# Layer 0 of a hybrid encoder: projections in split form, and additions and products given to GpSimd

## The chip, the cores and the metric

The kernel runs on one core of a Trainium2 chip. The core's engines work side by side, each on its own queue of instructions in a fixed order: TensorE (PE in the profile, with its weight loads as PEld) does matrix products, VectorE (DVE) and ScalarE (ACT) work element by element, GpSimd (POOL) can do so too and issues DMAs, SyncE (SP) issues DMAs. An instruction waits at the head of its engine's queue until what it needs is there, and everything behind it waits with it. The metric is the device time of one execution in microseconds (us); lower is better.

## The reference

Two layers over 272 tokens (16 meta tokens and 256 of the input), width 2048. Layer 0 is where the change lies.

```python
for layer in range(DEPTH):                      # 2
    hn = rms_norm(h, mix_norm[layer])
    proj = hn @ w_in[layer]                     # 2048 -> 512 + 256 + 64 + 1024
    c_q, c_kv, k_rope, u = jnp.split(proj, splits, axis=-1)
    att = mla_attention(c_q, c_kv, k_rope, ...) # 8 heads; c_q, c_kv are normed first
    ssm = s5_mixer(u, ...)                      # 64 groups of 16, 64 complex states, both ways
    mixed = jnp.concatenate([rms_norm(att, ...), rms_norm(ssm, ...)], axis=-1)
    h = h + mixed @ w_out[layer]
    hn = rms_norm(h, ffn_norm[layer])
    h = h + (swiglu(hn, ...) if layer % 2 == 0 else moe_swiglu(hn, ...))
...
def rms_norm(x, g):
    y = xf * lax.rsqrt(jnp.mean(xf * xf, axis=-1, keepdims=True) + EPS)
    return (y * g).astype(x.dtype)
```

All data are float32, and the result has to be near that precision.

## The kernel before, in words

Everything is kept transposed: a tile has 128 features on the partitions and the 272 tokens along the row. `h` is 16 such tiles. A matrix product of width 128 out runs over 16 weight tiles of 128x128, which come in blocks of eight (512 KB, one DMA by SyncE) through the class `Stream`.

A product has one of two forms. In the **raw form** the float32 block itself is the weight: one float32 matmul for each weight tile, which the trace shows as two instructions (`bank<-fa,raw`). In the **split form** the block is taken apart first: `Stream.high` rounds it on ScalarE into `wh` (type float32r), `Stream.low` takes the rest on VectorE into `wl`; the input is taken apart in the same way into `XH` and `XL`, and each weight tile then costs three float32r matmuls, `XH,wh`, `XL,wh` and `XH,wl` (the loop in `gemm`). Before the change the first 40 blocks of layer 0 (`NRAW`) are raw: all of the input projection and of the latents' projections. The rest of the kernel is in split form.

Layer 0's mixer (`mixer(0, ...)`) goes like this.

- **Prologue.** For each of the 16 tiles of `h`, ScalarE writes `X0` (h times the norm's gain) and the square of h (`sq_acc`); TensorE multiplies `X0` with the first two output tiles' weights and adds the square to a sum over all features with a product by a matrix of ones (`bank<-sqr,ones`). The sum gives `r_in`, by which every projection is scaled afterwards.
- **Projections.** 15 output tiles: 8 for `u` (two of them done in the prologue), 4 for c_q, 2 for c_kv, 1 for k_rope. In the text they are tile 1 to tile 15. `u` goes by GpSimd's DMAs to DRAM (`uscr`) and comes back in another layout.
- **S5.** `prep` works out powers of lambda on VectorE and transposes them on TensorE into `Wp`. `v_all` makes 16 batches of V: GpSimd issues three loads for a batch (two from `pscr`, one from `ssm_bT`), two batches ahead in a ring of three, VectorE makes V in four operations (`v_make`), TensorE multiplies V with `u` (`ssm_x`, 128x136 in the trace, four instructions for a group, 32 groups in all). Then `ssm_scan` runs 66 steps on VectorE. `w_all` makes 32 batches of W: five products and differences with `Wp` and one closing operation on VectorE, then a small product on TensorE (`toep`, shown as eight instructions with out 128x96 or 64x96) and three short additions. GpSimd loads `ssm_C` and `ssm_bz` for them.
- **The rest.** Heads and attention, the first half of `w_out`, the S5 output, the gated product (GLU) with its own sum of squares, the second half of `w_out`.

The order of all instructions is fixed when the kernel is built: generators hand out work, and a planner (`Model`, `Sched`) with costs for TensorE, VectorE, ScalarE and the DMAs decides when each is due by its own clock. `yield "w0"` means: go on when VectorE is at most 1350 ns ahead of TensorE by that clock. What the planner assumed wrongly shows as a wait in the queues.

## Time and profile before

| what | value |
|---|---|
| median of 3 runs | 2502.1 us (2499.97 to 2502.74) |
| profiled execution, its time | 2502.09 us |
| its span, first to last instruction | 2500.3 us |
| TensorE busy | 2424.5 us (97%) |
| VectorE busy | 1902.1 us (76%) |
| ScalarE busy | 1397.1 us (56%) |
| GpSimd busy | 151.4 us (6%) |

The profiled execution is the span and 1.8 us around it, and it stands at the median of the runs. Busy shares are over the whole span. Layer 0's mixer is the first seventh of it.

### The profile page before, as it was taken

The numbers are of one execution on the slowest core, as the hardware profiler recorded it, in microseconds if no ns is written. First come the engines' busy times: TensorE is split into PE (matmuls) and PEld (weight loads), VectorE is DVE, ScalarE is ACT, GpSimd is POOL, SyncE is SP. The second block draws the span as 40 slices with busy tenths as digits, with TensorE's granted clock in tenths as the row PEclk, the third lists the DMA queues.
The fourth block names the chain that finished last, engine by engine and source line by source line (L and its number), as shares of the span: only waits on it lengthen the run. The fifth ranks groups of instructions, "written<-read, shape, count | busy, mean of one in ns | idle before, by whom it ended". The sixth has DMA issues, their size and how long they took to land. (4 is left out here: it accounts for less than half of the span.)

```text
span 2500.3 us, 42271 instructions
## 1 busy us (share of the span) xinstructions
PE 2424.5 (97%) x15930; PEld 2189.2 (88%) x15930; DVE 1902.1 (76%) x3250; ACT 1397.1 (56%) x1908; POOL 151.4 (6%) x262
## 2 busy tenths in 40 slices
PE   8899999999999999999999899999999999999997
PEld 6675699999999999999998769997888888888886
DVE  8788667787766666555653887658999999999997
ACT  4424555443333333333458456646777877877775
POOL 3400100011100000000011002000000000000000
PEclk9999999999999999999999899999999999999998
DMA  7842554478765655555565316557999999999995
GB/s 257 238 145 83 155 155 160 161 223 273 245 197 189 193 190 176 184 169 177 178 199 174 125 44 220 220 191 263 391 351 352 383 340 375 363 329 373 362 336 198
DMA packets 192919, 583.47 MB, mean 233 GB/s; under 512 B 36225, under 2 KB 48897, under 8 KB 191553
## 3 DMA queue, kind: packets, MB, share of 16 engines
q1 hardware_dynamic: 174802, 520.42, 59.7%
q0 software_dynamic: 17040, 57.97, 7.6%
q8 instruction: 127, 2.08, 0.3%
q10 hardware_dynamic: 864, 2.28, 0.3%
q14 instruction: 86, 0.70, 0.1%
HBM read 560.14 MB, written 22.54 MB: 233 GB/s over the span
## 5 line engine op out<-in xcount | busy, mean ns | idle before, releaser
L408 DVE TENSOR_TENSOR wl<-raw,wh 128x1024 fp32r<-128x1024 f32 (+1 forms) x559 | 667.3, 1202 | 222.9 <-ACT wh L408 198.1
L408 ACT ACTIVATE wh<-raw 128x1024 fp32r<-128x1024 f32 (+1 forms) x559 | 579.4, 1040 | 309.6 <-PE bank L408 223.6
L408 PE MATMUL bank<-XH,wh 128*128 128x272 f32 (+1 forms) x2160 | 639.0, 296 | 0.8 <-ACT tmpr L408 0.5
L408 PE MATMUL bank<-XH,wl 128*128 128x272 f32 (+1 forms) x2160 | 624.7, 289 | 3.5 <-DVE wl L408 3.5
L408 PE MATMUL bank<-XL,wh 128*128 128x272 f32 (+1 forms) x2160 | 623.3, 289 | 1.5 <-DVE XL L408 1.3
L408 PEld LDWEIGHTS bank<-XH,wh 128*128 128x128 f32 x2160 | 410.1, 190 | 5.4 <-ACT tmpr L408 0.7
L408 PEld LDWEIGHTS bank<-XH,wl 128*128 128x128 f32 x2160 | 409.4, 190 | 4.2 <-DVE wl L408 4.2
L408 PEld LDWEIGHTS bank<-XL,wh 128*128 128x128 f32 x2160 | 410.2, 190 | 2.5 <-DVE XL L408 2.1
L408 PE MATMUL bank<-ra,wh 128*128 128x272 f32 (+1 forms) x1792 | 344.7, 292 | 2.3 <-ACT wh L408 2.3
L408 PEld LDWEIGHTS bank<-ra,wh 128*128 128x128 f32 x1792 | 283.7, 190 | 7.8 <-issue 3.1
L408 PE MATMUL bank<-fa 128*68 128x64 f32 (+11 forms) x1892 | 254.6, 273 | 30.7 <-DMA fa<-uscr 10.9
L408 PEld LDWEIGHTS bank<-fa 128*68 128x68 f32 (+6 forms) x1892 | 190.7, 157 | 88.6 <-issue 50.2
L408 DVE TENSOR_TENSOR fa<-fa 128x128 f32<-128x128 f32 (+9 forms) x687 | 236.3, 353 | 39.3 <-ACT fa L408 16.5
L408 PE MATMUL bank<-ra,wl 128*128 128x272 f32 (+1 forms) x896 | 258.4, 288 | 0.7 <-DVE wl L408 0.7
L408 ACT ACTIVATE fa<-bank 64x268 f32<-64x268 f32 (+9 forms) x313 | 159.3, 515 | 155.1 <-PE bank L408 136.2
L408 PE MATMUL bank<-wh,XH 128*128 128x512 f32 (+1 forms) x584 | 222.7, 381 | 0.4 <-ACT fa L408 0.4
L408 PE MATMUL bank<-wh,XL 128*128 128x512 f32 (+1 forms) x584 | 220.3, 377 | 0.0
L408 PE MATMUL bank<-wl,XH 128*128 128x512 f32 (+1 forms) x584 | 219.2, 375 | 0.0
L408 PE MATMUL bank<-wh,ra 128*128 128x512 f32 x552 | 185.1, 392 | 0.0
L408 PEld LDWEIGHTS bank<-ra,wl 128*128 128x128 f32 x896 | 170.4, 190 | 1.0 <-DVE wl L408 1.0
L408 PE MATMUL bank<-fa,raw 128*128 128x272 f32 x608 | 162.0, 404 | 7.8 <-DMA raw<-w_mix 6.3
L408 DVE TENSOR_TENSOR wl<-h,wh 128x1024 fp32r<-128x1024 f32 (+1 forms) x137 | 157.0, 1156 | 10.0 <-ACT wh L408 7.4
(127 smaller groups left out, 3211.3 us busy)
## 6 DMA issues: line engine op xcount, KB each, us to landing
raw<-w_dense SPq DMA_DIRECT2D x264, 512.0 KB, 3.6
raw<-w_mix SPq DMA_DIRECT2D x150, 512.0 KB, 3.8
raw<-w_moe_g SPq DMA_DIRECT2D x106, 512.0 KB, 5.6
h<-w_moe_g SPq DMA_DIRECT2D x80, 512.0 KB, 7.1
raw<-w_moe_d SPq DMA_DIRECT2D x73, 512.0 KB, 6.9
h<-w_moe_d SPq DMA_DIRECT2D x59, 512.0 KB, 6.7
raw<-w_moe_t SPq DMA_DIRECT2D x51, 384.0 KB, 4.0
h<-w_moe_t SPq DMA_DIRECT2D x44, 384.0 KB, 4.0
```

What stands on the lines that cost most here:

```text
L408: return f(*a, **k)
```

## The change

`NRAW = 40` becomes a list, `RAW`: blocks 0 to 5 (tiles 1 to 3) and 30 to 39 (the projections out of the latents, with the heads) stay raw, blocks 6 to 29 (tiles 4 to 15) are split. So ScalarE now rounds `X0` into `XH` and GpSimd takes the rest into `XL`, 16 operations each (`parts`), and 24 weight blocks are taken apart. The squares of h are no longer summed by TensorE one by one: GpSimd adds them into `wacc` (`joiner`), and one product with ones follows (`total`). In the same way VectorE joins the squares of the two latents and of the GLU's result. The five products and differences that make a batch of W go from VectorE to GpSimd; the closing operation and the three short additions stay (`VT`). The planner gets a time for GpSimd's operations, `pool_cost`, and the turn `"pool"`: go on when GpSimd is at most 1500 ns ahead. The DMAs that GpSimd issues are still planned on another clock.

```diff
-NRAW = 40
+RAW = list(range(6)) + list(range(30, 40))
...
+def pool_cost(name, a, k):
+    return 250.0 + 2.2 * size(a[0])
...
         self.gpsimd = Eng(nc.gpsimd, m, "pool", None)
+        self.pool = Eng(nc.gpsimd, m, "POOL", pool_cost)
...
+        if w == "pool":
+            return self.m.t["POOL"] < self.now() + 1500.0
...
-            out += [(ap[i], ap.shape[2], n == "w_mix0" and i < NRAW) for i in range(ap.shape[0])]
+            out += [(ap[i], ap.shape[2], n == "w_mix0" and i in RAW) for i in range(ap.shape[0])]
...
             if k:
-                self.nc.vector.tensor_tensor(acc, acc, s, op=OP.add)
+                self.joiner.tensor_tensor(acc, acc, s, op=OP.add)
...
-        TT = nc.vector.tensor_tensor
+        TT = (nc.vector if l else nc.pool).tensor_tensor
+        VT = nc.vector.tensor_tensor
+        turn = "w1" if l else "pool"
...
-            yield f"w{l}"
+            yield turn
             TT(w[:, 0], p(0), cc(0), op=OP.mult)
...
+            X0 = E.get([KD, L])
+            low = []
+
+            def parts():
+                yield lambda: self.nsum >= KD
+                for k in range(KD):
+                    nc.scalar.activation(XH[:, k], X0[:, k], AF.Copy)
+                    yield self.rdy(XH[:, k])
+                    yield "pool"
+                    nc.pool.tensor_tensor(XL[:, k], X0[:, k], XH[:, k].bitcast(F32), op=OP.subtract)
+                    low.append(k)
+
+            add(parts())
+            self.joiner = nc.pool
             for k in range(KD):
                 nc.scalar.activation(X0[:, k], self.h[:, k], AF.Copy, scale=self.gain(0, "mix", k))
-                self.sq_acc(self.nps, self.h[:, k], D, k, KD)
+                self.sq_acc(self.nps, self.h[:, k], D, k, KD, wacc)
...
+                if raw and i == 2:
+                    yield from self.gemm(ps, KD, *pair(X0, None))
+                    yield lambda: len(low) == KD
+                    X0.free()
+                    st["accs"] = [E.get([L]) for _ in range(2)]
+                else:
+                    yield from self.gemm(ps, KD, *x)
...
-        acc = None if raw else self.Wt[:, BLK:]
+        acc = wacc if raw else self.Wt[:, BLK:]
```

How the queues move is seen at three places.

TensorE at the end of the prologue, before (`fa,raw` with bank_65 and bank_66 are tiles 1 and 2, bank_67 is tile 3, `cst,fa` are prep's transposes):

```order
L408 MATMUL bank_66<-fa,raw_99 128x272
L408 MATMUL bank_69<-cst,fa 128x64 x4
L408 MATMUL bank_72<-sqr,ones 128x272
L408 MATMUL bank_65<-fa,raw_99 128x272
L408 MATMUL bank_66<-fa,raw_99 128x272
L408 MATMUL bank_67<-fa,raw_100 128x272 x8
L408 MATMUL bank_67<-fa,raw_96 128x272 x8
L408 MATMUL bank_65<-fa,raw_97 128x272 x4
```

and in the change:

```order
L409 MATMUL bank_65<-fa,raw_99 128x272
L409 MATMUL bank_66<-fa,raw_99 128x272
L409 MATMUL bank_72<-Wp,ones 128x272
L409 MATMUL bank_67<-fa,raw_100 128x272 x8
L409 MATMUL bank_67<-fa,raw_96 128x272 x8
L409 MATMUL bank_68<-cst,fa 128x64 x8
L409 MATMUL bank_69<-cst,fa 128x64 x4
L409 MATMUL bank_65<-XH,wh_101 128x272
```

One product with ones (`Wp,ones`, the sum that GpSimd has joined) stands ahead of tile 3, prep's transposes moved behind it, and tile 4 follows in split form.

GpSimd from its last memset on, before:

```order
L778 MEMSET Wp 128x1280
L390 DMA pscr_73<-fa 32x4x256 x2
L390 DMA fa<-pscr_73 64x1x512 x2
L390 DMA fa<-ssm_bT 128x1x512
L390 DMA fa<-pscr_73 64x1x512 x2
```

and in the change:

```order
L409 TENSOR_TENSOR Wp<-Wp,sqr 128x272 x15
L391 DMA pscr_73<-fa 32x4x256 x2
L409 TENSOR_TENSOR XL<-fa,XH 128x272 x8
L391 DMA uscr_75<-fa 128x272 x2
L409 TENSOR_TENSOR XL<-fa,XH 128x272 x6
L391 DMA fa<-uscr_75 64x8x68 x2
L409 TENSOR_TENSOR XL<-fa,XH 128x272 x2
L391 DMA uscr_75<-fa 128x272
L391 DMA fa<-pscr_73 64x1x512 x2
L391 DMA fa<-ssm_bT 128x1x512
```

V's first loads (`fa<-pscr`, `fa<-ssm_bT`) now stand behind the 15 joins, the 16 subtractions and the first five DMAs for `u`.

GpSimd later, while V is made, before:

```order
L390 DMA fa<-pscr_73 64x1x512 x2
L390 DMA fa<-ssm_bT 128x1x512
L390 DMA fa<-ssm_bz 128x256
L390 DMA fa<-pscr_73 64x1x512 x2
L390 DMA fa<-ssm_bT 128x1x512
L390 DMA uscr_75<-fa 128x272
```

and in the change:

```order
L391 DMA fa<-pscr_73 64x1x512 x2
L391 DMA fa<-ssm_bT 128x1x512
L409 TENSOR_TENSOR fa<-Wp,fa 128x192 x2
L391 DMA fa<-pscr_73 64x1x512 x2
L391 DMA fa<-ssm_bT 128x1x512
L391 DMA fa<-ssm_bz 128x256
L409 TENSOR_TENSOR fa<-Wp,fa 128x192 x2
L409 TENSOR_TENSOR fa<-fa 128x192
L409 TENSOR_TENSOR fa<-Wp,fa 128x192 x2
```

Operations for W (`fa<-Wp,fa`, `fa<-fa`) stand between the loads for V. From V's first load to its last the queue holds 75 DMAs (88 before) and 60 of these operations (none before). On TensorE, 140 of the 192 split weight tiles, 13 of the 32 `toep` products and all 32 groups of `ssm_x` stand between tile 3 and the last of `ssm_x`; 52 weight tiles, 5 `toep` and the sums of the two latents follow until tile 15 ends, and 14 `toep` stand later, among the heads. Before, it was 21 `toep` up to tile 15's end, three of them after the last of `ssm_x`, and 11 later.

## Rows read from the trace of the kernel before

**Rows 1.** The page: the span, and TensorE's busy time, share, instructions.
```profile
span 2500.3 us, 42271 instructions
...
PE 2424.5 (97%) x15930; PEld 2189.2 (88%) x15930; DVE 1902.1 (76%) x3250; ACT 1397.1 (56%) x1908; POOL 151.4 (6%) x262
```

**Rows 2.** Stretches of 25 us: length, PE, PEld, DVE, ACT, POOL busy, clock, DMA share, GB/s.
```profile
50.00:75.00 25.00, 22.69 (x138) 18.48 (x138) 21.08 (x65) 15.08 (x26) 14.19 (x26) 1.00 0.82 239
100.00:125.00 25.00, 21.83 (x129) 17.32 (x128) 20.90 (x64) 11.35 (x22) 11.41 (x21) 1.00 0.84 246
```

**Rows 3.** TensorE in order of time, first 43 us: start us, length us, what.
```profile
6.29 2.15 PE L408 MATMUL bank<-fa,raw 128*128 128x272 f32 x4 [6.29 <-DMA raw<-w_mix]
...
32.26 10.25 PE L408 MATMUL bank<-fa,raw 128*128 128x272 f32 x44
42.43 0.88 PE L408 MATMUL bank<-fa 128*64 128x96 f32 x8
```

**Rows 4.** ScalarE in order of time, the prologue.
```profile
22.34 0.72 ACT L408 ACTIVATE fa<-fa 64x256 f32<-64x256 f32 x2 [3.66 <-DVE fa L408]
...
24.20 0.51 ACT L408 ACTIVATE fa<-h,gn 128x272 f32<-128x272 f32 x1
...
27.55 0.41 ACT L408 ACTIVATE sqr<-h 128x272 f32<-128x272 f32 x1
```

**Rows 5.** VectorE in order of time: prep's products, the scan's first and last step.
```profile
17.30 12.00 DVE L408 TENSOR_TENSOR fa<-fa 64x128 f32<-64x128 f32 x32
...
137.71 0.48 DVE L408 TENSOR_TENSOR fa<-L,fa 128x128 f32<-128x128 f32 x2
...
236.19 0.61 DVE L408 TENSOR_TENSOR fa<-fa 128x128 f32<-128x128 f32 x2
```

**Rows 6.** GpSimd in order of time: first and last load for V.
```profile
27.25 0.52 POOL L390 DMA_DIRECT2D fa<-pscr  x1 [1.49 <-DMA pscr<-fa]
...
125.21 0.55 POOL L390 DMA_DIRECT2D fa<-ssm_bT  x1 [1.75 <-PE bank L408]
```

**Rows 7.** TensorE in order of time, from tile 4 to the attention's end.
```profile
47.49 1.51 PE L408 MATMUL bank<-fa 128*128 128x136 f32 x12 [1.69 <-DMA fa<-uscr]
...
132.78 1.59 PE L408 MATMUL bank<-fa 128*128 128x136 f32 x12 [2.26 <-DVE fa L408]
...
134.87 0.63 PE L408 MATMUL bank<-fa 128*128 128x136 f32 x4
...
177.75 7.04 PE L408 MATMUL bank<-fa,raw 128*128 128x272 f32 x30
...
290.62 1.66 PE L408 MATMUL bank<-sqr,ones 128*128 128x272 f32 x6
```

**Rows 8.** TensorE in order of time: the split form's step from one weight tile on.
```profile
299.30 0.29 PE L408 MATMUL bank<-XH,wh 128*128 128x272 f32 x1
...
300.81 0.29 PE L408 MATMUL bank<-XH,wh 128*128 128x272 f32 x1
```

**Rows 9.** Groups of instructions, 0 to 400 us: xcount | busy us, mean ns | idle before.
```profile
L408 DVE TENSOR_TENSOR fa<-Wp,fa 128x192 f32<-128x192 f32 x128 | 40.8, 348 | 6.0 <-DMA wscr<-fa 4.2 <-DMA uscr<-fa 1.9
L408 DVE TENSOR_TENSOR wl<-raw,wh 128x1024 fp32r<-128x1024 f32 x26 | 31.8, 1224 | 6.2 <-ACT wh L408 5.6
...
L390 POOL DMA_DIRECT2D fa<-pscr x32 | 16.7, 536 | 5.9 <-DVE fa L408 2.5 <-DMA pscr<-fa 1.9 <-DMA fa<-pscr 0.7
...
L390 POOL DMA_DIRECT2D fa<-uscr x16 | 11.2, 706 | 13.9 <-DMA uscr<-fa 8.9 <-issue 5.0
...
L956 POOL MEMSET fa<- 128x1088 f32 x2 | 1.9, 1004 | 0.3 <-POOLq L2379 0.3
...
L2379 POOL MEMSET const-float32-1.0<- 128x1 f32 x1 | 0.1, 101 | 0.0
```

**Rows 10.** DMA issues, 25 to 130 us: xcount, KB each, median us to landing.
```profile
fa<-pscr POOLq DMA_DIRECT2D x32, 128.0 KB, 4.8
uscr<-fa POOLq DMA_DIRECT2D x8, 136.0 KB, 4.9
```

More of the change, by code (lines that the diff above doesn't have):

```diff
@@ L245 @@
 class Model:
-    OUT = {"PE": 197.0, "DVE": 127.0, "ACT": 152.0, "DMA": 960.0}
+    OUT = {"PE": 197.0, "DVE": 127.0, "ACT": 152.0, "POOL": 200.0, "DMA": 960.0}
     def __init__(self):
-        self.t = {"PE": 0.0, "DVE": 0.0, "ACT": 0.0, "DGE": 0.0, "DMA": 0.0}
+        self.t = {"PE": 0.0, "DVE": 0.0, "ACT": 0.0, "POOL": 0.0, "DGE": 0.0, "DMA": 0.0}
         self.q = {}
@@ L772, in start @@
         nc, A = self.nc, self.A
+        self.joiner = nc.vector
         self.eye = self.cst[:, CE:CE + 16]
@@ L1174, in toep @@
             q = Dd.ap
-            TT(e[0:16, :, 0], e[0:16, :, 0], e[32:48, :, S - 1], op=OP.add)
-            TT(q, dd, ey, op=OP.mult)
-            TT(e[0:16, :, 0], e[0:16, :, 0], q, op=OP.add)
+            VT(e[0:16, :, 0], e[0:16, :, 0], e[32:48, :, S - 1], op=OP.add)
+            VT(q, dd, ey, op=OP.mult)
+            VT(e[0:16, :, 0], e[0:16, :, 0], q, op=OP.add)
             def store():
@@ L1215, in cc @@
                 return c[:, :, r, :].rearrange("p (o g) c -> p o g c", o=1).to_broadcast(sh)
-            yield f"w{l}"
+            yield turn
             TT(w[:, 0], p(0), cc(0), op=OP.mult)
-            yield f"w{l}"
+            yield turn
             TT(t.ap, p(1), cc(1), op=OP.mult)
-            yield f"w{l}"
+            yield turn
             TT(w[:, 0], w[:, 0], t.ap, op=OP.subtract)
-            yield f"w{l}"
+            yield turn
             TT(w[:, 1], p(0), cc(1), op=OP.mult)
-            yield f"w{l}"
+            yield turn
             TT(t.ap, p(1), cc(0), op=OP.mult)
-            yield f"w{l}"
+            yield turn
             nc.vector.scalar_tensor_tensor(w[:, 1], w[:, 1], -1.0, t.ap, op0=OP.mult, op1=OP.subtract)
@@ L1413, in mixer @@
         st["accs"] = None if raw else [F.get([L]) for _ in range(2)]
+        wacc = self.Wt[:, 2 * (TC + 2) * NG:][:, :L]
         cqf, ckf = F.get([4, N]), F.get([2, L])
-        st["acc"] = acc = None if raw else st["accs"][0].ap
+        st["acc"] = None if raw else st["accs"][0].ap
         r_in = F.get([L])
@@ L1422, in pair @@
             return lambda k: h[(slice(None), k) + s], None if l is None else lambda k: l[(slice(None), k) + s]
-        if raw:
-            X0 = E.get([KD, L])
-            x, xq = pair(X0, None), pair(X0, None)
-        else:
-            x, xq = pair(XH, XL), pair(XH, XL, slice(q0, L))
+        x, xq = pair(XH, XL), pair(XH, XL, slice(q0, L))
         def put_u(T, ue):
@@ L1447, in mixer @@
                 yield None
+            while self.pend and self.pend[0][0].__name__ != "total":
+                self.flush(len(self.pend) - 1)
+            self.joiner = nc.vector
         add(self.norm(self.nps, L, r_in.ap, ("r_in", l)))
@@ L1454, in u_tile @@
                 ps = self.psum("m")[:, :L]
-                yield from self.gemm(ps, KD, *x)
+                if raw and i == 2:
[5 more added lines that the diff above has]
+                    yield from self.gemm(ps, KD, *x)
             yield self.has("r_in", l)
@@ L1482, in mixer @@
             TT(cqf[:, m], ps, r_in[:, q0:], op=OP.mult)
-            self.sq_acc(nq, cqf[:, m], 512, m, 4, acc)
+            self.sq_acc(nq, cqf[:, m], 512, m, 4, st["accs"][0].ap)
         rq, rk = F.get([N]), F.get([L])
@@ L1492, in mixer @@
             yield self.has("root", "q", l)
-            self.sq_acc(nk, ckf[:, m], 256, m, 2, None if raw else st["accs"][1].ap)
+            self.sq_acc(nk, ckf[:, m], 256, m, 2, st["accs"][1].ap)
         add(self.latent(l, nk, L, ckf.ap, ap(ckh), ap(ckl), "kv", 2, rk.ap))
@@ L1496, in mixer @@
         yield from self.gemm(ps, KD, *x)
-        if raw:
-            X0.free()
         kr = E.get([L], top=True)
@@ L1502, in mixer @@
         yield self.has("kv", l)
-        for t in (rq, rk, r_in) + (() if raw else (cqf, ckf)):
+        for t in (rq, rk, r_in) + (tuple(st["accs"]) if raw else (cqf, ckf)):
             t.free()
@@ L1586, in mixer @@
             self.sq_acc(ns, t, 1024, m, 8, acc)
-        for t in [g, gh, gl] + (st["accs"] or []):
+        for t in [g, gh, gl] + ([] if raw else st["accs"]):
             t.free()
```

## The prediction

> **What bounds the kernel now.** I read the page first: TensorE is busy for 97% of the span, so time can be won only where it does less work or waits less [rows 1]. Then the stretches of layer 0. Between 50 and 125 us TensorE lacks 2 to 3 us in every 25, VectorE is busy for 84%, GpSimd for about half, the DMA engines for 82 to 84% [rows 2]. The reader should see a stage where TensorE leads but everything else is near full too. Third, TensorE in order of time: its waits there are for `u`'s way through DRAM and for VectorE (1.69, 2.26 us), the last product of `ssm_x` is at 134.87 us, and the row from 177.75 us holds the end of tile 15 in its first 15 instructions, so at 181.2 us [rows 7]. The attention ends near 292 us, while the scan on VectorE runs only from 137.7 to 236.8 us [rows 5, 7]: V and the scan may be 50 us later before anything waits for them, except TensorE itself, which takes V's products in a fixed order.
>
> **The change part by part.**
>
> *Split form.* 44 raw instructions take from 32.26 to 42.43 us, 0.231 each, so a raw weight tile costs 0.46 us [rows 3]. In split form four weight tiles take from 299.30 to 300.81 us, 0.378 each [rows 8]. For 192 weight tiles TensorE's work falls by 192 x 0.082 = 15.7 us. The price is 24 more `wl` at 1.22 us on VectorE, 29 us, while the W products that leave it are 128 of 0.35 us and 32 like them, about 50 us with the overlap taken off [rows 9]; VectorE ends with less to do, and I cost it at nothing. If V's products were late on VectorE instead, TensorE would wait there as it does at 132.78 us [rows 7].
>
> *Sums of squares.* 26 products with ones go, 15 in the prologue, 4 among the latents, 7 in the GLU: 26 x 0.46 = 12 us of TensorE. The 11 joins on VectorE that replace the last 11 cost 0.4 us each beside TensorE's work.
>
> *GpSimd's price.* No row shows an operation of two inputs on GpSimd. From below: its memset writes 1088 elements in 1004 ns, 0.92 ns each, and a memset of one element takes 101 ns, so 192 elements with one stream take 0.28 us [rows 9]. From above: three streams (two read, one written) at that rate, 0.63 us, and if each operation also has to wait for one of VectorE's (0.5 us for a product for V, by four in 2 us), 1.13 us. I take 0.75: near 0.63, since only memory traffic is sure, and a quarter of the way to the upper end, since VectorE is busy for 84% there and three of a batch's five wait for the one in front. For 272 elements the same three-stream sum gives 0.85 us. The Trainium skill, GPSIMD Engine Reference, section Performance versus the Vector engine, measures 4497 ns for a tensor_tensor of 2048 elements; scaled, an estimate of 0.42 us for 192, with which V's stage below would be 20 us shorter and the sum 2461 us.
>
> *Prologue.* TensorE's own work shrinks from 48 to 33 products. It then hangs on ScalarE, which idled 3.66 us for VectorE and copied prep's powers between two squares, from 18.68 to 24.20 us [rows 4]. Those copies now come after the squares, so the last square ends 5.5 us sooner, at 22.4 instead of 27.96 us. GpSimd's last join follows at 23.5, the sum at 23.7, and tile 3 runs from 23.7 to 31.1 us instead of from 32.26. Then TensorE meets prep's transposes, moved behind tile 3. VectorE's prep products ended at 29.3 us [rows 5]; ahead of the last six now stand a reciprocal, two products for `u` and two `wl`, 5.3 us. Transposes at 34.6, tile 4 from 35.7 us. On GpSimd: two DMAs for prep, 8 subtractions, two stores of `u`, 6 subtractions, two loads of `u` (which wait 4.9 us for the store to land [rows 10]), 2 subtractions: `XL` is complete at 41.5 us, when TensorE needs it at about 41.0. What is late next is V: its first load, at 27.25 us before [rows 6], goes out at 42.1 us.
>
> *V's stage.* GpSimd's queue decides it. From V's first load to the last stand 75 DMAs of 0.55 us and six of these 0.15 us longer [rows 9], 42 us, and 60 operations at 0.75 us, 45 us. Last load at 42.1 + 87 = 129.1 us (125.2 before [rows 6]); 4.8 us to land [rows 10], 2 us of VectorE, 0.9 us of TensorE: `ssm_x` ends at 136.8 us, against 135.4 before. TensorE's own work to that point would be done sooner: 35.7 + 140 x 0.378 + 32 x 0.46 + 13 x 0.8 (`toep`) = 113.7 us. So it waits 23 us here, mostly in front of V's products, and what split form saves in this stage is given back.
>
> *After V.* Before, 87.5 raw weight tiles, 6 sums and 3 `toep` took from 135.4 to 181.2 us. Now 52 split weight tiles, 2 sums and 5 `toep` remain: 19.7 + 0.9 + 4.0 = 24.6 us, so tile 15 ends at 161.4 us, 19.8 us sooner. W's last 17 batches cost GpSimd 17 x (5 x 0.75 + 0.55) = 73 us from 129 us, done near 202 us; from tile 15 to the attention's end TensorE took 111 us [rows 7], and the last `toep` stands at about three fifths of that stretch in the new order, near 227 us, so nothing waits for W. Three more `toep` among the heads than before cost 2.4 us, the GLU's 7 products save 3.2 us.
>
> *Sum:* -19.8 + 2.4 - 3.2 = -20.6 us. The profiled execution took 2502.09 us, which is the median of the runs, so 2481 us.
>
> **The rivals.**
>
> *GpSimd keeps up.* At 0.35 us an operation, what VectorE needs for it now [rows 9], V's stage takes 24 us less, and TensorE's own work is the bound: `ssm_x` ends near 115 us, 2459 us. For it: the low price may be real, and the DMAs in the queue are fewer than before. Against: DMA engines at 84% [rows 2] must carry the same loads in less time.
>
> *GpSimd and VectorE hold each other up.* This one ends slower. At 1.13 us, V's stage is 23 us longer; and VectorE's prep, whose products stand without a gap from 17.30 us [rows 5], would be pushed back by the 15 joins, some 5 us. `ssm_x` ends at 165 us, tile 15 at 189 us: 2508 us, and more if VectorE's products for V stretch as well. It decides from about 1.0 us an operation, where the 20.6 us are gone. For it: VectorE has no idle time into which GpSimd's reads could fall. Against: no row shows the two engines reading side by side. Beside this: the Trainium skill, SBUF — State Buffer, section Who interferes with whom, says that a VectorE instruction with two SBUF inputs contends with a GpSimd instruction that reads SBUF; by that rule this rival holds in part, and no run so far shows how much.
>
> *Loads queue behind waits.* GpSimd's operations wait for W's stores to land and for VectorE's closing operation, and V's loads stand behind them. At 1 us for each of the 13 batches in V's stage, 2494 us. W's products on VectorE waited 6.0 us in all for such stores [rows 9], which speaks for a smaller price.
>
> **How the numbers follow.** Forecast 0.43, GpSimd keeps up 0.2, waits 0.15, contention 0.22. 0.2% of 2502 us is 5 us, about what a measurement of this kernel can tell from no change. The first two are faster whole, of the waits 0.1 and of contention none: 0.73. Same: 0.05 of the waits and 0.06 of contention, 0.11. Slower: the other 0.16. The low end of the range, 2463, leaves out the fastest part of GpSimd keeping up; the high end, 2508, is contention at its price.
>
> **What the next profile would show.** Right: GpSimd's operations for W spaced 0.6 to 0.9 us; tile 3 begins near 24 us; V's first load near 42 us and last near 129 us; TensorE waits some 20 us between, most of it for V; tile 15 ends near 161 us; the heads and everything after them as before but earlier. Wrong: a spacing under 0.5 us with `ssm_x` done before 120 us; a spacing over 1 us, prep's products longer than 12 us; or VectorE, busier than now, as the engine for which TensorE waits.

## The result and the profile after

The changed kernel takes 2532.5 us (median of 4 runs, 2528.0 to 2536.7) against 2502.4 us: ratio 1.0122, 95% interval 1.0098 to 1.0146. It is 30 us slower; 20 us less were forecast. The page after, to be set against [rows 1]:

```profile
span 2534.0 us, 42724 instructions
...
PE 2428.8 (96%) x16070; PEld 2200.6 (87%) x16070; DVE 1940.0 (77%) x3125; ACT 1428.1 (56%) x1948; POOL 286.3 (11%) x453
```

160 operations have left VectorE and 35 have come to it (24 `wl`, 11 joins). By the prediction's prices that is some 16 us less to do; it is busy for 38 us longer. The stretches of layer 0 after, columns as in [rows 2]:

```profile
25.00:50.00 25.00, 13.73 (x64) 11.18 (x63) 24.28 (x38) 11.17 (x25) 19.08 (x24) 0.79 0.50 160
50.00:75.00 25.00, 22.64 (x153) 21.61 (x152) 17.31 (x31) 10.80 (x14) 19.98 (x33) 0.87 0.75 234
100.00:125.00 25.00, 21.10 (x146) 19.13 (x146) 20.64 (x35) 15.19 (x24) 24.71 (x40) 0.92 0.83 229
150.00:175.00 25.00, 22.11 (x152) 20.37 (x151) 24.06 (x51) 12.64 (x23) 18.30 (x29) 0.89 0.46 140
```

GpSimd is full between 100 and 125 us; VectorE is full between 25 and 50 and from 150 us on. VectorE's third number needs care. The same stretch from 150 us of the kernel before:

```profile
150.00:175.00 25.00, 25.00 (x115) 20.35 (x114) 23.96 (x91) 2.10 (x5) 0.54 (x1) 1.00 0.47 148
```

VectorE is as busy before as after, with 91 instructions against 51. In part the mix differs: 20 of the 51 are operations of the scan on 128x128, 72 of the 91 were, and four are long `wl`. In part the instructions are stretched, as the groups below show. TensorE after, in order of time: the end of tiles 1 and 2, tile 3, prep's transposes after a wait, the first split product, `ssm_x`'s last product, tile 15's last, the attention's last sums, the GLU's last product:

```profile
17.74 10.21 PE L409 MATMUL bank<-fa,raw 128*128 128x272 f32 x36 [1.89 <-ACT fa L409]
...
28.24 7.50 PE L409 MATMUL bank<-fa,raw 128*128 128x272 f32 x32
...
45.44 0.80 PE L409 MATMUL bank<-cst,fa 64*128 64x64 f32 x5 [9.37 <-DVE fa L409]
...
48.75 0.59 PE L409 MATMUL bank<-XH,wh 128*128 128x272 f32 x1
...
156.43 0.63 PE L409 MATMUL bank<-fa 128*128 128x136 f32 x4
...
190.10 0.29 PE L409 MATMUL bank<-XH,wl 128*128 128x272 f32 x1
...
323.07 1.66 PE L409 MATMUL bank<-sqr,ones 128*128 128x272 f32 x6
...
428.03 0.29 PE L409 MATMUL bank<-ra,wl 128*128 128x272 f32 x1
```

Tile 3 is done at 35.7 us; then TensorE waits 9.4 us for prep on VectorE. Why prep is late stands on the two engines' rows side by side, GpSimd first (joins, `XL`, first and last load for V), then VectorE (prep, the scan's first and last step):

```profile
6.59 0.76 POOL L409 TENSOR_TENSOR Wp<-Wp,sqr 128x272 f32<-128x272 f32 x1 [2.05 <-ACT sqr L409]
...
18.15 7.89 POOL L409 TENSOR_TENSOR Wp<-Wp,sqr 128x272 f32<-128x272 f32 x9 [3.46 <-ACT sqr L409]
...
32.78 6.83 POOL L409 TENSOR_TENSOR XL<-fa,XH 128x272 fp32r<-128x272 f32 x8
...
52.71 1.03 POOL L391 DMA_DIRECT2D fa<-pscr  x2 [0.30 <-issue]
...
145.71 0.59 POOL L391 DMA_DIRECT2D fa<-ssm_bT  x1
```

```profile
6.76 0.60 DVE L409 SCALAR_TENSOR_TENSOR fa<-fa 64x2 f32<-64x2 f32 x1
...
21.79 13.60 DVE L409 TENSOR_TENSOR fa<-fa 64x128 f32<-64x128 f32 x26
...
42.62 5.45 DVE L409 TENSOR_TENSOR fa<-fa 64x256 f32<-64x256 f32 x6
...
159.26 0.47 DVE L409 TENSOR_TENSOR fa<-L,fa 128x128 f32<-128x128 f32 x2
...
318.56 0.61 DVE L409 TENSOR_TENSOR fa<-fa 128x128 f32<-128x128 f32 x2
```

The reader should see the first row of each. GpSimd's first join runs from 6.59 to 7.35 us; VectorE's operation on 64x2 elements, 0.15 us for the same one before, begins inside it and ends at 7.36, with it. Prep's products on 64x128 take 0.42 us in the mean (0.27 before), those on 64x256 0.67 us (0.42 before). The scan ended at 236.8 us [rows 5] and now ends at 319.2. The groups to 345 us (count | busy, mean ns | idle):

```profile
L409 DVE TENSOR_TENSOR fa<-fa 128x128 f32<-128x128 f32 x132 | 45.1, 341 | 2.3
L409 DVE TENSOR_TENSOR fa<-L,fa 128x128 f32<-128x128 f32 x132 | 42.6, 362 | 0.6
L409 DVE TENSOR_TENSOR wl<-raw,wh 128x1024 fp32r<-128x1024 f32 x28 | 38.5, 1379 | 3.1 <-ACT wh L409 3.1
L409 DVE TENSOR_TENSOR fa<-fa 128x512 f32<-128x512 f32 x32 | 25.1, 784 | 3.2 <-DMA fa<-ssm_bT 2.8
L409 DVE TENSOR_TENSOR fa<-fa 16x32 f32<-16x32 f32 x64 | 20.1, 314 | 1.8
```

```profile
L409 POOL TENSOR_TENSOR fa<-Wp,fa 128x192 f32<-128x192 f32 x128 | 83.5, 669 | 23.3 <-DVE fa L409 20.9 <-DMA wscr<-fa 1.9
L409 POOL TENSOR_TENSOR fa<-fa 128x192 f32<-128x192 f32 x32 | 25.4, 792 | 2.5
```

Before, the means of VectorE's five were 287, 284, 1220, 687 and 179 ns. With the other groups whose means rose the stretch adds up to 54 us, as much as the W products (about 50 us by the prediction) had cost there. Some 14 us of it stand before 50 us, in prep and in two `wl`; 17 us in the scan's steps; 12 in W's short additions; 7 in V's products. The same shows within the one trace: of the scan's 132 products with `L`, the 42 that run beside a GpSimd sum for more than half of their time take 529 ns in the mean, the other 90 take 284.

TensorE's clock is the second thing to see. Columns as in [rows 2], the clock is the last number but two. The kernel before, from tile 15's end to the attention's end and from the start to there:

```profile
181.20:292.30 111.10, 108.82 (x488) 66.17 (x487) 86.15 (x335) 53.33 (x151) 9.49 (x17) 0.98 0.31 90
0.00:292.30 292.30, 270.79 (x1316) 196.17 (x1317) 237.42 (x841) 121.15 (x287) 66.03 (x121) 0.99 0.55 168
```

After, the wait for prep and what follows it, then the same two stretches:

```profile
39.30:53.00 13.70, 5.67 (x28) 5.36 (x29) 13.16 (x20) 1.74 (x4) 11.32 (x15) 0.50 0.38 120
190.40:324.70 134.30, 124.00 (x508) 72.43 (x508) 111.23 (x394) 54.82 (x154) 48.46 (x83) 0.90 0.34 99
0.00:324.70 324.70, 277.17 (x1470) 209.91 (x1471) 273.04 (x709) 151.93 (x327) 201.85 (x314) 0.89 0.53 161
```

Up to the attention's end TensorE waits 48 us instead of 22. It is also busy for 6 us longer, though by the prediction's prices it has some 24 us less to do there. For 59 of its busy us the granted clock was 0.5, the lower of its two levels (1.2 GHz; the full one is 2.4), before the change for 7. The three longest stretches at 0.5 began in or behind a wait of TensorE, of 9.4, 2.7 and 1.6 us. Split products stand 0.227 us apart at the lower level and 0.126 at the full one, so the lower clock cost some 23 us up to there (an estimate: 52 us more at 0.5, times the share that a split product loses).

### The profile page after: what moved, and what is told of

Its sections match the earlier page's. It is cut to its first block, busy times and chain, and to the rows that moved or that the text cites. A ratio compares the mean times of both kernels' runs of the same rounds, so it can differ in the third digit from the quotient of the medians.

```text
span 2534.0 us, 42724 instructions
## 1 busy us (share of the span) xinstructions
PE 2428.8 (96%) x16070; PEld 2200.6 (87%) x16070; DVE 1940.0 (77%) x3125; ACT 1428.1 (56%) x1948; POOL 286.3 (11%) x453
## 5 line engine op out<-in xcount | busy, mean ns | idle before, releaser
L409 PE MATMUL bank<-XH,wh 128*128 128x272 f32 (+1 forms) x2352 | 704.4, 299 | 0.5 <-ACT tmpr L409 0.5
L409 PE MATMUL bank<-XH,wl 128*128 128x272 f32 (+1 forms) x2352 | 684.1, 291 | 7.7 <-DVE wl L409 7.7
L409 PE MATMUL bank<-XL,wh 128*128 128x272 f32 (+1 forms) x2352 | 682.2, 290 | 1.6 <-DVE XL L409 1.3
L409 PEld LDWEIGHTS bank<-XH,wh 128*128 128x128 f32 x2352 | 450.6, 192 | 7.4 <-issue 0.9
L409 PEld LDWEIGHTS bank<-XL,wh 128*128 128x128 f32 x2352 | 450.6, 192 | 2.7 <-DVE XL L409 2.2
L409 PE MATMUL bank<-fa 128*68 128x64 f32 (+10 forms) x1892 | 271.9, 282 | 40.4 <-ACT fa L409 13.8
L409 PEld LDWEIGHTS bank<-fa 128*68 128x68 f32 (+5 forms) x1892 | 197.0, 162 | 103.1 <-issue 41.7
L409 DVE TENSOR_TENSOR fa<-fa 128x128 f32<-128x128 f32 (+10 forms) x655 | 255.9, 400 | 26.2 <-ACT fa L409 10.6
L409 ACT ACTIVATE fa<-bank 64x268 f32<-64x268 f32 (+8 forms) x313 | 160.6, 518 | 123.6 <-PE bank L409 114.5
L409 ACT ACTIVATE fa<-fa 128x272 f32<-128x272 f32 (+6 forms) x142 | 86.0, 617 | 145.1 <-DVE fa L409 139.9
```

Source lines behind the costliest of these rows:

```text
L409: return f(*a, **k)
```

## The experiments

One table first, since most readings are of it. In us: where `ssm_x`'s last product ends, the last `toep`, the scan's last product with `L`, the attention's last sum, and the GLU's last product. From there to the end of the span all of these kernels need 2097 to 2108 us. Ratios are against runs of the kernel before on the same chip; its medians on these chips lie between 2501.7 and 2505.0 us, so that a difference of a few us between medians of different rows says little.

| kernel | median | ratio, 95% interval | ssm_x | toep | scan | attention | GLU |
|---|---|---|---|---|---|---|---|
| before | 2502.4 | | 135.5 | 285 | 236 | 292.3 | 398.6 |
| full change | 2532.5 | 1.0122 (1.0098–1.0146) | 157.1 | 276 | 319 | 324.7 | 428.3 |
| 1: W on VectorE | 2538.1 | 1.0141 (1.0114–1.0169) | 138.2 | 363 | 292 | 255.4 | 429.7 |
| 2: joins, XL on VectorE | 2518.4 | 1.0063 (1.0044–1.0082) | 163.1 | 267 | 306 | 309.4 | 412.5 |
| 3: 1 and 2 | 2527.7 | 1.0096 (1.0070–1.0122) | 143.9 | 360 | 311 | 260.4 | 430.5 |
| 4: before, W on GpSimd | 2537.8 | 1.0145 (1.0119–1.0171) | 155.5 | 226 | 275 | 329.5 | 436.2 |
| 5: before, shadow sums | 2540.5 | 1.0162 (1.0135–1.0189) | 158.3 | 323 | 267 | 329.8 | 435.3 |
| 6: before, shadow memsets | 2539.2 | 1.0147 (1.0123–1.0171) | 173.1 | 327 | 274 | 333.4 | 442.5 |
| 7: 2, W after V | 2503.0 | 1.0003 (0.9988–1.0019) | 135.2 | 320 | 290 | 294.1 | 401.3 |
| 8: full, low parts cut | 2524.9 | 1.0104 (1.0081–1.0128) | 154.4 | 266 | 308 | 317.0 | 419.8 |
| 9: full, W after V | 2524.1 | 1.0091 (1.0070–1.0113) | 123.2 | 314 | 292 | 318.8 | 420.9 |
| 10: 7, low parts cut | 2503.7 | 1.0009 (0.9992–1.0025) | 133.5 | 321 | 291 | 295.7 | 402.9 |
| 11: 4, W after V | 2534.4 | 1.0134 (1.0113–1.0155) | 125.8 | 296 | 265 | 326.8 | 433.5 |
| 12: 7, W whole on GpSimd | 2503.7 | 1.0007 (0.9991–1.0023) | 134.5 | 343 | 278 | 284.0 | 401.6 |
| 13: full, V's DMAs on SyncE | 2518.3 | 1.0057 (1.0036–1.0079) | 146.0 | 248 | 301 | 310.6 | 414.2 |
| 14: 2, V's DMAs on SyncE | 2506.9 | 1.0019 (1.0005–1.0032) | 159.7 | 255 | 297 | 299.4 | 402.1 |
| 15: 3, W first | 2508.3 | 1.0030 (1.0019–1.0041) | 194.9 | 208 | 331 | 304.3 | 405.5 |
| 16: before, sums joined | 2501.9 | 0.9995 (0.9979–1.0010) | 138.0 | 288 | 240 | 292.2 | 393.2 |
| 17: 15, low parts cut | 2507.4 | 1.0015 (0.9999–1.0031) | 193.5 | 207 | 331 | 304.0 | 405.1 |
| 18: 3, W between | 2515.7 | 1.0051 (1.0033–1.0068) | 205.9 | 204 | 324 | 315.6 | 416.8 |

**1 to 4: the parts of the change.** W back on VectorE (1), joins and `XL` on VectorE (2), both (3); in 4 the W edit alone, in the kernel before:

```diff
-        TT = (nc.vector if l else nc.pool).tensor_tensor    # 1, 3
-        turn = "w1" if l else "pool"
+        TT = nc.vector.tensor_tensor
+        turn = f"w{l}"
-                    nc.pool.tensor_tensor(XL[:, k], X0[:, k], ...)    # 2, 3
+                    nc.vector.tensor_tensor(XL[:, k], X0[:, k], ...)
-            self.joiner = nc.pool
+            self.joiner = nc.vector
```

> The full change with layer 0's W products back on VectorE; the joins of h's squares and XL stay on GpSimd. Theory 1 (sharing: while a GpSimd operation of two inputs runs, VectorE's operations are held, about 0.3 us for each): the prologue keeps its 13 us (tile 4 near 48.7 us, prep's last product near 48 us), but the 160 operations for W stop stretching VectorE, whose 128x128 steps of the scan go back to 0.28 us; VectorE does 45 us of W itself instead of 40 us of stretch, so little is won: 2505 to 2525 us. Theory 2 (GpSimd's queue delays V's loads): the last load for V follows the first by about 45 us instead of 93, ssm_x ends before 130 us, and the time falls to 2480 to 2495 us. Theory 3 (split form itself costs, by 24 more low parts on VectorE and high parts on ScalarE): still near 2530 us.

> The full change with the joins of h's squares and XL's subtractions on VectorE; W stays on GpSimd. Theory 1 (sharing): VectorE's prep is not stretched any more, but VectorE does 31 operations of 0.42 us itself, 13 us, which is what the stretch was worth, so tile 4 starts no more than 5 us sooner and the time is 2522 to 2532 us. Theory 2 (GpSimd's queue): 27 us of arithmetic leave the queue ahead of V's loads, the first of them goes out near 40 us instead of 52.7 and the time falls by about 10 us, to 2515 to 2522. Theory 3 (split form itself): near 2530 us.

> The split form, the latents and the joins as in the full change, but no arithmetic on GpSimd: joins, XL and W on VectorE. Theory 1 (sharing): no stretch anywhere (scan steps 0.28 us), but VectorE has 13 us more in the prologue and 29 us more of low parts than the kernel before; 2500 to 2520 us, better than the full change by 10 to 30 us. Theory 2 (GpSimd's queue): V's loads go out as before, 2480 to 2495. Theory 3 (split form itself): no better than the full change, 2525 us or more.

> The kernel before with nothing but layer 0's W products moved to GpSimd (raw form, ones-products as before). Theory 1 (sharing): 160 operations stretch VectorE by about 40 us where W's products had cost it 45, the scan's 128x128 steps rise from 0.28 to about 0.35 us, the time is 2500 to 2515 us. Theory 2 (GpSimd's queue): V's loads stand behind the operations, last load for V near 125 to 130 us, as before; no change, 2500 us. Theory 3 (split form itself is to blame): the time of the kernel before or less, 2490 to 2502.

Runs 1, 3 and 4 lie at or above the highest range given. Run 2 lies in that of the queue (2515 to 2522), but not for its reason: V's first load goes out at 56.0 us, later than in the full change (52.7). Its first split product stands at 33.46 us instead of 48.75; VectorE does `XL` itself there, 8 in 2.90 us where GpSimd took 6.83, and prep's transposes now stand behind 57 split weight tiles, three and a half output tiles, where none stood ahead of them. Prep itself ends no sooner on VectorE (53.4 us, 48.1 in the full change):

```profile
33.46 0.49 PE L409 MATMUL bank<-XH,wh 128*128 128x272 f32 x1
```

```profile
25.56 2.90 DVE L409 TENSOR_TENSOR XL<-fa,XH 128x272 fp32r<-128x272 f32 x8
```

Run 4 says that split form isn't needed for the loss: W on GpSimd alone costs 36 us. Runs 1 and 3 say that giving W back to VectorE (1), or all of the arithmetic (3), doesn't win them back: the attention ends 32 to 37 us sooner than before, but VectorE takes W last, `toep` ends at 360 us, and from 300 to 375 us TensorE is busy for 44 of 75 us in either, at a granted clock of 0.57 and 0.61.

**5 and 6: GpSimd's reads, or its queue?** The kernel before, with one unused GpSimd operation beside each of W's five on VectorE, 160 in all; in 5 a product of two tables, in 6 two memsets of 720 elements together:

```diff
+            nc.gpsimd.tensor_tensor(z[:, :192], zc[:, :192], zc[:, 256:448], op=OP.mult)    # 5
+            nc.gpsimd.memset(z, 1.0)    # 6
+            nc.gpsimd.memset(z[:, :208], 1.0)
```

> The kernel before, and behind each of W's five products and sums on VectorE one GpSimd operation of two inputs (128x192, from the constants, result unused), 160 in all; VectorE and TensorE have the same work as before. Theory 1 (sharing): VectorE's operations of two inputs are held while one of these runs, the means of groups rise (128x128 from 0.28 to about 0.35 us, 128x512 from 0.69 to 0.78), some 40 us more on VectorE, and the time rises to 2515 to 2540 us, well over the run with writes only. Theory 2 (GpSimd's queue): V's loads are late by what stands ahead of them in the queue, whatever the operation reads: the same rise as in the run with writes only, and VectorE's means stay.

> The kernel before, and at the same 160 places two GpSimd memsets of 512 and 208 elements instead (720 elements at 0.92 ns, an estimate of 0.66 to 0.8 us for the pair, so the queue is as full as with the operation of two inputs, but nothing is read). Theory 1 (sharing of reads): VectorE's means stay as in the kernel before, and the time rises only by the queue, to 2500 to 2512 us. Theory 2 (queue): as slow as the run with two inputs.

The same time twice, by different means. Groups to 345 us of run 5, VectorE and GpSimd:

```profile
L408 DVE TENSOR_TENSOR fa<-Wp,fa 128x192 f32<-128x192 f32 x128 | 57.6, 478 | 0.0
...
L408 DVE TENSOR_TENSOR fa<-fa 16x32 f32<-16x32 f32 x64 | 24.6, 384 | 4.1 <-ACT fa L408 2.2
...
L408 DVE TENSOR_TENSOR fa<-bank,fa 128x272 f32<-128x272 f32 x15 | 7.9, 535 | 0.1
```

```profile
L1159 POOL TENSOR_TENSOR Wp<-cst 128x192 f32<-128x192 f32 x160 | 109.5, 684 | 10.0
```

And of run 6:

```profile
L408 DVE TENSOR_TENSOR fa<-Wp,fa 128x192 f32<-128x192 f32 x128 | 40.8, 348 | 3.0 <-DMA wscr<-fa 3.0
...
L408 DVE TENSOR_TENSOR fa<-fa 16x32 f32<-16x32 f32 x64 | 11.5, 180 | 20.9 <-ACT fa L408 19.0
...
L408 DVE TENSOR_TENSOR fa<-bank,fa 128x272 f32<-128x272 f32 x15 | 8.0, 537 | 3.5 <-PE bank L408 3.4
```

```profile
L1159 POOL MEMSET Wp<- 128x512 f32 x160 | 85.8, 536 | 6.9
L1160 POOL MEMSET Wp<- 128x208 f32 x160 | 43.5, 272 | 9.2
```

With GpSimd reading, VectorE's operations of two SBUF inputs grow by 55 us in nine groups (W 348 to 478 ns); a group that reads one of its inputs from PSUM (`bank,fa`) stays at 535. With GpSimd only writing, the means of all these groups stay as before. So GpSimd's reads do hold VectorE up. But run 6 loses as much without this hold: V's loads stand behind the memsets, and `ssm_x` ends 38 us late. The queue alone is thus enough for a loss of this size. Run 5 has the hold and the queue together, and its sums fill the queue for 110 us, run 6's memsets for 129, so the pair doesn't say what the hold costs by itself. Run 11 below takes the queue out.

**13 and 14: V's DMAs out of the queue.** V's loads, `u`'s stores and its loads issued by SyncE; GpSimd's arithmetic unchanged:

```diff
-        self.nc.gpsimd.dma_start(bt.rearrange(...), ...)
+        (self.nc.gpsimd if l else self.nc.sync).dma_start(bt.rearrange(...), ...)
```

> The full change with layer 0's loads for V, u's stores and u's loads issued by SyncE instead of GpSimd, so that they no longer stand behind joins, XL and W. Theory 1 (queue): V's loads go out as buffers come free, ssm_x ends near 135 us instead of 157, the time falls by 10 to 20 us, 2512 to 2523. Theory 2 (GpSimd holds VectorE up, which is then late with V's products): V's stage stays, 2527 us or more. If SyncE's weight loads are pushed back by these DMAs, TensorE waits for raw and the time is over 2535.

> The run with 2518 us (joins and XL on VectorE, W on GpSimd from the start) with the same DMAs on SyncE. Theory 1 (queue): it gains what holding W back gained, 15 us, and W also ends earlier, beside V's stage, so that less of it holds up the scan: 2490 to 2503. Theory 2 (VectorE held up): 2512 to 2520.

Taking these DMAs out of GpSimd's queue is worth 14 us in the full change (2532.5 to 2518.3) and 11 in run 2's kernel, as much as moving joins and `XL` (14 and 11). `ssm_x` ends 11 us sooner in 13. In 14 it ends only 3 us sooner; there the last `toep` ends at 255 instead of 267 us, and the attention 10 us sooner.

**7, 9, 11: W held until V is through.**

```diff
+        if l == 0:
+            yield lambda: self.st.get("vn", 0) >= 16
         for b in range(NB):
...
-        yield lambda: "rh" in st and self.R is not None and ...    # 7 and 9, not 11
+        yield lambda: "rh" in st and (l or "rw" in st) and self.R is not None and ...
```

The second line, which 10, 12 and 16 have too, lets layer 0's S5 output take its buffers only after those for W's loads; no run has it alone.

> The full change with joins and XL on VectorE (as in the run with 2518 us), and W on GpSimd held until the last product of ssm_x, so that no GpSimd arithmetic runs beside V and none stands ahead of V's loads. Theory A (VectorE bounds, by its own work and by what GpSimd's operations hold it up): V's stage runs full, ssm_x ends near 120 us instead of 158, the stretch moves to the scan; W's 32 batches at about 4.3 us take until 260 us; the time is 2495 to 2512. Theory B (GpSimd's queue is the bound): V's stage gets its 35 us back and the time falls below 2490. If W then ends last (toep after 290 us), 2515 or more.

> The full change (joins and XL on GpSimd, as in the change) with nothing but W held until the last product of ssm_x. Theory A (two separate costs that add: some 14 us of the prologue, where GpSimd's joins and XL hold VectorE's prep up, and some 15 us of V's stage, where GpSimd's operations stand ahead of V's loads): the prologue's 14 us stay and V's 15 go, 2512 to 2520 us. Theory B (one bound, GpSimd's queue in the whole of layer 0, so that the first late load only shifts the rest): most of the 30 us go, 2500 to 2510. If W is not what delays V's loads, 2526 or more.

> The kernel before with W on GpSimd, as in the run with 2538 us, and W held until the last product of ssm_x; raw form and ones-products as before. Theory A (GpSimd's operations ahead of V's loads made that run's 36 us): ssm_x ends near 130 us again instead of 155, W runs beside the scan and ends near 280 us, 2500 to 2512 us. Theory B (GpSimd's hold on VectorE made them): the hold is the same length, now beside the scan; 2525 to 2540.

Run 7 is back at the kernel before, 30 us under the full change. Run 9 keeps 21 us of them, and 7 and 9 differ only by where joins and `XL` are done. Run 11 tells most: `ssm_x` is through 10 us sooner than in the kernel before, so V's loads behind GpSimd's sums are out of it, and the loss is still 1.3%, 29 us against the median on its own chip. Its stretch from 150 us, what TensorE waited for from 120 to 300 us (in total, times, longest), and what ScalarE's squares waited for up to 235 us:

```profile
150.00:175.00 25.00, 20.61 (x104) 15.82 (x103) 24.24 (x71) 2.42 (x7) 15.52 (x28) 1.00 0.50 149
```

```profile
PE bank L408 <- ACT sqr L408: 12.0, 5, 3.4
PE bank L408 <- DVE fa L408: 5.3, 6, 1.6
```

```profile
ACT sqr L408 <- DVE fa L408: 33.6, 5, 8.7
```

VectorE is full, with 71 instructions where the kernel before has 91; its scan steps are stretched to 377 and 380 ns. TensorE's ones-products wait for ScalarE's squares, and these for what VectorE takes out of TensorE's banks between the scan's steps. In the kernel before the squares wait for VectorE as long (31.3 us), but no ones-product of TensorE waits for them there. Up to the attention's end TensorE waits 44 us in run 11, 22 before, and is busy for 24 us at a clock of 0.5, 7 before. W's products also stand later, and VectorE's closing operation waits 10.2 us for GpSimd; that the stretch alone makes the loss is argued from these rows, not tried by itself.

**8, 10, 17: the low parts.** Layer 0's 24 `wl` computed for 16 of 1024 columns, in the full change, in run 7's kernel and in run 15's:

```diff
-            self.nc.vector.tensor_tensor(self.ring(1, i), self.src(i), ...)
...
+            n = 16 if i < 40 else o.shape[-1]
...
+            V.eng.tensor_tensor(o[:, :n], x[:, :n], y[:, :n], op=OP.subtract)
...
+        for t in self.S.wl:
+            nc.gpsimd.memset(t.bitcast(F32), 0.0)
```

> The full change, but the low parts of layer 0's 24 split weight blocks are computed for 16 of 1024 columns only (the other columns stay zero; left out is that part of the subtraction, the products with wl are still done). It takes some 25 us from VectorE and nothing else. Theory A (VectorE is what bounds layer 0 after the change): the time falls by 12 to 28 us, to 2504 to 2520. Theory B (GpSimd's queue and the rest bound it; the 24 low parts lie in VectorE's idle time, as the prediction costed them): within 6 us of the full change, 2526 to 2538.

> The run with 2503 us (joins and XL on VectorE, W on GpSimd after V), with the low parts of the 24 split blocks computed for 16 of 1024 columns only (left out: the rest of that subtraction; three memsets on GpSimd at the start fill the columns). Theory A (with the queue out of the way VectorE bounds layer 0: it is busy 24 of 25 us from 150 to 250 us): 25 us of VectorE give 10 to 22 us, 2481 to 2493. Theory B (TensorE's own work and W's end on GpSimd bound): within 5 us, 2498 to 2508.

> The kernel without GpSimd arithmetic and with W ahead (2508 us), with the low parts of the 24 split blocks computed for 16 of 1024 columns only (left out: the rest of that subtraction; three memsets on GpSimd at the start fill the columns). Theory A (the 24 low parts fill VectorE, for which TensorE waits from 100 to 200 us): 24 x 1.06 us leave VectorE where it is full, ssm_x ends 18 to 25 us sooner than at 195 us, and the time falls to 2484 to 2494 us, under the kernel before. Theory B (the low parts are covered, W and V alone fill VectorE there): 2503 to 2512 us.

The planner still counts the whole subtraction, so the order stays. Some 24 us less on VectorE give 7.6 us in the full change, where the intervals of the two ratios overlap, and nothing in the other two. The three memsets cost something themselves: beside them one TENSOR_SCALAR of VectorE on 64x2 takes 4.0 to 5.0 us instead of 1.3 to 1.5, and the first split product stands 3 to 4 us later. So some 3 us of gain may be hidden in each of the three. Run 10 couldn't tell what it was meant to, since the 24 blocks are through before VectorE is full; run 17 takes them where VectorE was full, and there, too, they are covered. What paces run 17 from 125 to 200 us is then W and V in turn, GpSimd's queue waiting for TensorE's products, mostly with W's load `ssm_bz` at its head, ahead of V's loads (here 125 to 200 us):

```profile
POOL fa L394 <- PE bank L412: 40.2, 17, 6.0
```

**12, 15, 18: other places for W.** In 12 its closing operation goes to GpSimd too (ScalarE negates C's imaginary part); in 15 and 18 W, on VectorE, may run 5000 or 2500 ns ahead of TensorE instead of 1350:

```diff
-            nc.vector.scalar_tensor_tensor(w[:, 1], w[:, 1], -1.0, t.ap, op0=OP.mult, op1=OP.subtract)    # 12
+            TT(w[:, 1], w[:, 1], t.ap, op=OP.subtract)
-LEAD = {"prep0": 800.0, "v0": 1200.0, "w0": 1350.0, ...    # 15, 18
+LEAD = {"prep0": 800.0, "v0": 1200.0, "w0": 5000.0, ...
```

> The run with 2503 us with W's closing operation on GpSimd too (ScalarE negates C's imaginary part once for 8 groups, so that the closing operation is a plain difference): 32 operations of 0.36 us leave VectorE, 32 of 0.67 us come to GpSimd, and GpSimd no longer waits for VectorE between two batches (48 us of waits in that run). Theory A (W's end and VectorE's full queue bound it): W ends some 25 us sooner, the last toep near 295 us, 2488 to 2498 us. Theory B (a GpSimd operation costs VectorE as much as it saves): no change, 2499 to 2508.

> The run without arithmetic on GpSimd (2528 us), with W's products taken sooner by VectorE (the planner lets them run ahead of TensorE by 5000 ns instead of 1350). Theory A (VectorE's whole work up to Y is the bound, some 60 us more than before by low parts, joins and XL): W ends sooner, but the scan, the attention's products and the low parts end later by as much; 2518 to 2535. Theory B (only the order was bad): W ends before 300 us, 2485 to 2505.

> The same kernel without GpSimd arithmetic, all low parts computed, W ahead of TensorE by 2500 ns instead of 5000 or 1350. If VectorE's whole work up to Y bounds it, the place of W only trades ssm_x's end against W's end: 2503 to 2515 us, no better than the kernel before. If the two orders each lose by waits that an order between avoids: 2490 to 2500.

Run 12 changes nothing (its second theory): W's end even moves from 320 to 343 us. Run 15 lies between its theories: 19 us of run 3's loss were the order, the rest stays; `ssm_x` ends 59 us late, the scan with it. No place of W brings the kernel under the one before.

**16: sums joined alone.**

```diff
-        acc = None if raw else self.Wt[:, BLK:]
+        acc = wacc if raw else self.Wt[:, BLK:]
```

(and the same for the latents' two sums)

> The kernel before with nothing but the sums of squares of the latents and of the GLU joined on VectorE (13 products with ones less, 11 sums of 272 elements more on VectorE); raw form, W on VectorE, nothing on GpSimd. By the prediction's price of 0.46 us a product, TensorE has 5 us less work: 2495 to 2499 us if nothing else bounds there. Theory A (VectorE bounds layer 0 up to Y, TensorE the GLU): the GLU's 3 us come, the latents' 2 us do not: 2497 to 2501.

The edit takes away 11 products with ones (the expectation says 13), 5 us at the prediction's price. The GLU's last product ends 5.4 us sooner: 3.2 us within the GLU, 2.2 between the attention and the GLU, and none up to the attention's end, where the latents' products went. The time doesn't show it (12 runs from 2493.6 to 2507.3 us), 2.4 us of it are gone again by the end of the profiled execution. Of all runs this is the nearest to a version that beats the kernel before, and it doesn't.

## Why the prediction was wrong

The range ended at 2508 us and slower had 0.16. Point by point, forecast and measured:

- **GpSimd's price was right.** 0.75 us forecast, 0.669 and 0.792 measured for W, 0.80 for a join and 0.93 for `XL` (forecast 0.85). The rival that keeps up is out. V's stage went by the forecast's rule: from its first load to its last 93 us, 87 forecast. The 6 us more are waits of the queue, which the sum had left out and the rival of loads behind waits had put at 13. That W's sums in the queue set this stage, runs 1 and 9 show: without them it takes 69 and 58 us.
- **The step that failed: "VectorE ends with less to do, and I cost it at nothing."** W's 50 us did leave, but GpSimd's operations, W's with the joins and `XL`, lengthened VectorE's own by 54 us. This is the rival of the two engines holding each other up, named with 0.22, and mis-sized twice. It was tied to a GpSimd price above 1 us and bounded at 2508; the hold falls on VectorE, at a GpSimd price under 0.8 us. And what was priced was V's stage and 5 us in prep; V's products stretched by 7 of the 54 us, prep with its two `wl` by 14, and the scan and W's additions, which had no price, by 29.
- **Prologue.** The last join ended at 26.0 us (23.5 forecast), tile 3 at 35.7 (31.1), and the first split product stands at 48.75 instead of 35.7 us. Joins and `XL` held prep up: the 5.3 us of work put ahead of its last six products were counted, the stretch of 14 us was not. V's first load went out at 52.7, not 42.1 us, and `ssm_x` ended at 157.1 instead of 136.8 us. Without joins and `XL` on GpSimd, 14 us (run 2, from the full change) and 21 us (run 7, from run 9) come back. But not by a sooner prep, which ends at 53.4 us in both: there TensorE has 57 split weight tiles to do before it meets the transposes. What the hold and what the order of the queue is worth, these runs don't part.
- **After V.** Forecast: tile 15 at 161.4 us and the attention 113 us later. Measured: 190.4 us and 134 us later. The prediction said that "nothing waits for W", and gave V and the scan 50 us of room; the scan ended 82 us later. The 134 us are 23 more than in the kernel before. TensorE waits 10 us in them, 2 before; the lower clock, at which it was busy for 27 us there and for 3 before, makes some 11 more (an estimate as above). From the first scores to the attention's end the kernels without GpSimd arithmetic beside them need 81 to 91 us (before, 1, 3, 15 to 18), those with W on GpSimd beside them 94 to 124 us (the full change, 2, 7 to 14). Part of that is TensorE's own work, since the stretch holds from 0 (15, 17, 18) to 20 (7, 10) `toep` products of 0.8 us; with these taken off it is 76 to 87 against 85 to 108 us. Run 11, without split form, joins or a late V, stands at the low end, 85 us against 78 in the kernel before. Run 5, with unused sums beside the stretch, needs 93 us, and run 6, whose memsets stretch none of these operations, 90: not all of the lengthening is the hold.
- **24 low parts at nothing:** nearly right. 7.6 us in the full change, none in runs 10 and 17, with the 3 us of the memsets open.
- **Split form and sums.** The GLU's 3.2 us came (27.5 to 24.4 us from its first product to its last). The 15.7 us and the other sums were won as work and given back twice: as waits, which the prediction had for V's stage alone, and as a lower clock, which it didn't have at all. Its 0.378 us for a split weight tile is a step at full clock [rows 8]; three products 0.227 us apart are 0.68 us. In 7, 10 and 12 all 28 us of work are saved and none shows: up to the attention's end TensorE waits 32 to 35 us there and is busy for 33 to 49 us at a clock of 0.5 (22 and 7 before).

In sum: 20 us of the miss stand at `ssm_x`'s end (11 of them at V's first load already), 9 more by tile 15, 21 in the attention, 4 after the GLU, where the profiled execution is itself 3.6 us above the median. The 30 us by tile 15 and in the attention divide between the hold on VectorE, W's closing operation, for which VectorE waited 14.5 us, and TensorE's clock; no run tells them apart. Run 12, without that wait on VectorE, won nothing, and no run held the clock up. What paces runs 15 and 17 between 125 and 200 us was only read from waits, not tried.

## What to carry to other kernels

Before work goes to an engine that seems idle, price it three times: its own duration, what it does to instructions that run beside it on the neighbour, and what stands behind it in that engine's queue. Here the first was right. The third alone was worth the whole loss in run 6; the second stretched VectorE by as much as the change had taken off it, and run 11 lost about as much with V's loads out of its way. A price read where an engine runs without waits has the clock of that place in it; waits that a change brings can take the clock with them. And a busy share tells how long instructions took, not what was done: VectorE's rose from 76 to 77% of the span with 125 instructions fewer.

## What the hardware showed

- GpSimd's operations that read two tensors hold up VectorE's two-input operations from SBUF, tiny ones most: 16x32 elements go from 180 to 384 ns in run 5. By 160 such operations of 0.68 us VectorE loses 55 us, 0.35 us each. Run 6's memsets, 0.81 us for a pair, hold none of these operations. The Trainium skill, SBUF — State Buffer, section Who interferes with whom, states just this, that a VectorE instruction with two SBUF inputs contends with a GpSimd instruction that reads SBUF, not with one that only writes it; runs 5 and 6 agree.
- A reciprocal of VectorE on 64x128 beside the joins takes 946 ns (945 before); three reductions from PSUM beside W's sums take 426 to 437 ns (435 before); in run 5 four copies from PSUM beside the sums take 434 ns (436 before). But TENSOR_SCALAR on 64x128, of one input, rises from 216 to 431 ns in the mean in the full change: the three that run beside joins take 780 to 802 ns, the other five 215. Memsets hold this operation too: on 64x2 it takes 0.16 us alone, 1.3 to 1.5 us beside the memset at the start, and 4.0 to 4.2 us beside the four of runs 10 and 17, until they are over. The same section of the Trainium skill says that tensor_scalar can contend in a two-port mode; no run here shows the mode.
- A wait can cost TensorE a second time: with the 9.4 us of waiting for prep the granted clock falls to 0.5, from 39.3 to 53.0 us, and the first split products stand 0.227 us apart until 52.8 us, then 0.126. Not every wait does this: in the kernel before TensorE waits for 19 us in all up to `ssm_x`'s end, and its clock is below full for 3.4 us there. What else lowers it stays open.
